# Split probabilities side by side: one product with the values per block of keys in a streaming attention kernel

## Chip, cores and metric

The kernel runs on one core of a Trainium2 chip. The metric is the device time of one execution in microseconds (us); a second time is the span of the profiled execution, from its first to its last instruction.

## What is computed

One layer of a streaming encoder, for 1024 new rows of a prompt group and 64 rows of a sample group, model width 1024, float32. One normalised input goes through one combined projection; three groups of heads share it (eight "forgetting attention" heads of width 64, a pooling mixer, four heads that attend to 256 memory tokens); gates and one output projection close the layer. Of the reference, the part that the change touches:

```python
def fox_attend(q, k, v, Fq, Fk, qpos, kpos):
    s = jnp.einsum('bqhd,bkhd->bhqk', q, k).astype(jnp.float32) * SCALE
    bias = jnp.transpose(Fq, (0, 2, 1))[..., :, None] - jnp.transpose(Fk, (0, 2, 1))[..., None, :]
    s = jnp.where(kpos[None, :] <= qpos[:, None], s + bias, NEG)
    p = jax.nn.softmax(s, axis=-1).astype(v.dtype)
    return jnp.einsum('bhqk,bkhd->bqhd', p, v)

def mem_attend(qm, mk, mv):
    s = jnp.einsum('bqhd,bkhd->bhqk', qm, mk).astype(jnp.float32) * SCALE
    p = jax.nn.softmax(s, axis=-1).astype(mv.dtype)
    return jnp.einsum('bhqk,bkhd->bqhd', p, mv)
```

## The kernel before

**Split numbers.** Products that need float32 accuracy are made of float32r operands: a high part (a rounded copy, made on ACT) and a low part (the rest, by a subtraction on DVE or GpSimd, POOL in the profile). A projection is three products per block (high by high, high by low, low by high), the `pp` accumulators of the profile with `xh`, `xl`, `whi`, `wlo`.

**Attention units.** A prompt head is worked in four units `fox_unit(h, c)` of 256 queries; unit c sees 256(c+1) keys. Scores go into `s`, softmax on DVE and ACT gives two probability tiles of 128 queries (`P` or `Q` by their width). Then, for each pair of key blocks `kp`, from the last down, TensorE transposes up to four 128x128 blocks into `pt`; `pt_split` makes the high part `phi` (ACT) and the low part `plo` (DVE); four products of 256 columns add up in the accumulator `o`. In the last pair (`kp == c`) the later key block lies wholly in the future of the first 128 queries: its transpose is left out, and two memsets on POOL put zeros there. The values `vs` hold their high part in one half of the 128 columns and their low part in the other, so one product gives both halves; `finish` adds the two halves of partitions (ACT copies one to `ot`, DVE adds) and stores the sum through `cat` to `catd` in memory. `mem_unit` does the same once per unit for the memory heads, with the values in `vm`. There are 8 x 4 prompt units with 1 to 4 pairs each (80 pairs, 32 of them last ones) and 4 x 4 memory units.

**Order.** Heads come in the order of a string, `f0 f1 f2 f3 m0 m1 m2 m3 f4 .. f7`, with projections of later tiles written behind each head as filler. A planner (`Planner`) takes the whole program, gives every operation a cost of its own (for a float32r product 0.008 us and 0.000435 us per column, at least 0.108), and writes out a fixed order for each engine by list scheduling: on TensorE, operations that write `s`, `pt` or `o` go first among those ready at one time. All engines then work their queues in that order. `q` and `k` of a pair of heads go through memory (`qd`, `kd`) and are loaded again (`qa`, `qb`, `ks`). When the last projection is done, `w_out` is loaded into the buffers of the split input, and the output projection runs over nine row tiles.

**Buffers.** PSUM: two each of `pp`, `s`, `pt`, `o`, one bank (512 float32 columns) each. In SBUF `phi`, `plo`, `ot` have two buffers, `cat` three. All loads and nearly all stores are issued by SP's queue.

In the trace nearly every instruction carries line 251, the line on which the planner emits; so one goes by tiles.

Of the kernel before, what the change touches and what calls it, by code (L numbers as in the profile page):

```python
# [7 lines left out]
F32 = mybir.dt.float32  # L8
F32R = mybir.dt.float32r
BF16 = mybir.dt.bfloat16  # L10
AF = mybir.ActivationFunctionType
ALU = mybir.AluOpType
AX = mybir.AxisListType

P = 128
# [256 lines left out]
def tile_hymba_step(  # L272
# [6 lines left out]
    nc = Planner(tc.nc, tc)  # L279
    PSUM = bass.MemoryType.PSUM  # L280

    def pool(name, bufs, space=None, to=ctx):
        kw = {} if space is None else {"space": space}
        return _Pool(nc, to.enter_context(tc.tile_pool(name=name, bufs=bufs, **kw)))
# [11 lines left out]
    def nm(s):  # L296
        uid[0] += 1
        return f"{s}_{uid[0]}"

    def pst():  # L300
        return ps.tile([P, 512], F32, tag="s", name=nm("s"))
# [10 lines left out]
    def otile():  # L312
        return po.tile([P, 512], F32, tag="o", name=nm("o"))

    def mm(out, lhsT, rhs, start, stop):
        nc.tensor.matmul(out, lhsT=lhsT, rhs=rhs, start=start, stop=stop)

    def half(par):
        return slice(64 * par, 64 * par + 64), slice(64 - 64 * par, 128 - 64 * par)
# [7 lines left out]
    catd = [dram.tile([D, 256 if c < 4 else NSA], F32, name=f"catd{c}") for c in range(5)]  # L327
# [138 lines left out]
    def vacc():  # L466
        vt_n[0] += 1
        return (ppt, pst, ppt, pst, otile, ptt, pst)[vt_n[0] % 7]()
# [183 lines left out]
    def small_halves():  # L652
        return sp.tile([P, 2, 512], F32R, tag="hm", name=nm("hm"), bufs=2)
# [36 lines left out]
    with st:  # L690
# [79 lines left out]
        for t, (wh, wl) in enumerate(wm):  # L770
            acc = vacc()
# [12 lines left out]
            hl = small_halves()  # L784
# [4 lines left out]
        for t in range(2):  # L789
            acc = vacc()  # L790
            c = slice(t * P, t * P + P)
# [19 lines left out]
    ap_ = pool("ap", 2)  # L811

    def small(shape, tag):
        return ap_.tile(shape, F32, tag=tag, name=nm(tag), bufs=6)
# [14 lines left out]
    def q_part(q, c):  # L829
        t = q[c in (2, 3)]  # L830
        c0, n = ((0, 256), (256, 256), (0, 256), (256, 256), (512, P))[c]
        return t[:, 0, c0 : c0 + n], t[:, 1, c0 : c0 + n]

    def score(out, q, qs, kst, ks0, n):
        mm(out, q[0][:, qs], kst[:, ks0 : ks0 + n], True, False)
        mm(out, q[1][:, qs], kst[:, ks0 : ks0 + n], False, True)

    def nbt(n):
        tag, w = ("nb", 512) if n <= 512 else ("nc", NPR)
        return ap_.tile([P, w], F32, tag=tag, name=nm(tag))  # L840

    def ptile(n=1024):
        tag, w, bufs = ("P", 512, 4) if n <= 512 else ("Q", 1024, 3)
        return ap_.tile([P, w], F32, tag=tag, name=nm(tag), bufs=bufs)

    def softmax_tail(Pt, m, rows, n, rs, src=None):
        nc.scalar.activation(
            Pt[:rows, :n], Pt[:rows, :n] if src is None else src, AF.Exp, bias=m,
            scale=-1.0 if src is None else 1.0, accum_out=rs[:rows],
        )  # L850
# [3 lines left out]
    def rs_col(c, head, i=0):  # L854
        return rsum[:, c, 12 * i + head : 12 * i + head + 1]
# [8 lines left out]
        nc.vector.tensor_copy(rt[:n, :m], tp[:n, :m])  # L864
        nc.sync.dma_start(rsd[c, :n, :m], rt[:n, :m])

    def pt_split(src, a, b):
        hi = ap_.tile([P, 512], F32R, tag="phi", name=nm("phi"))
        lo = ap_.tile([P, 512], F32R, tag="plo", name=nm("plo"))
        nc.scalar.copy(hi[:, a:b], src[:, a:b])  # L870
        nc.vector.tensor_tensor(lo[:, a:b], src[:, a:b], hi[:, a:b], op=ALU.subtract)
        return hi, lo

    def finish(acc, par, row0, t0, n):
        r, o = half(par)
        rows = slice(row0 + 64 * par, row0 + 64 * par + 64)
        t = ap_.tile([P, 256], F32, tag="ot", name=nm("ot"))
        nc.scalar.copy(t[r, :n], acc[o, :n])
        cat = ap_.tile([P, 256], F32, tag="cat", name=nm("cat"), bufs=3)
        nc.vector.tensor_tensor(cat[r, :n], acc[r, :n], t[r, :n], op=ALU.add)  # L880
        nc.sync.dma_start(catd[t0 // 256][rows, :n], cat[r, :n])

    def fox_load(h):
        par = h % 2
# [12 lines left out]
    def fox_unit(h, c, ks, vs, q):  # L897
        par = h % 2
        j = h // 2
        nk = 256 * (c + 1)  # L900
        nb = nbt(nk)
        r0 = 8 * c * (c + 1) + h * (2 * c + 2)
        nc.sync.dma_start(
            nb[:, :nk],
            gpd[r0 : r0 + 2 * c + 2, :].rearrange("t p -> (t p)").unsqueeze(0).to_broadcast([P, nk]),
        )
        bm = ap_.tile([P, P], F32, tag="bm", name=nm("bm"))
        nc.gpsimd.tensor_tensor(bm, nb[:, nk - 256 : nk - P], mask, op=ALU.add)
        nc.gpsimd.tensor_tensor(nb[:, nk - P : nk], nb[:, nk - P : nk], mask, op=ALU.add)
        q = q_part(q, c)  # L910
        pts = []
        for i in (0, 1):
            n = 256 * c + 128 * (i + 1)
            Pt = ptile(n)
            prev = BIG
            step = 320 if n == 640 else 512
            for a in range(0, n, step):
                w = min(step, n - a)
                wc = max(w, 256)
                s = pst()  # L920
                score(s[:, :wc], q, slice(P * i, P * i + P), ks, a, wc)
                d = n - P if i == 0 else n
                segs = [(a, min(a + w, d), nb)] if a < d else []
                if i == 0 and a + w == n:
                    segs.append((d, n, None))
                for b0, b1, src in segs:
                    m = small([P, 1], "m")
                    nc.vector.tensor_tensor_reduce(
                        out=Pt[:, b0:b1], in0=s[:, b0 - a : b1 - a],
                        in1=bm if src is None else nb[:, b0:b1],  # L930
                        scale=-1.0, scalar=prev, op0=ALU.add, op1=ALU.min, accum_out=m,
                    )
                    prev = m
            softmax_tail(Pt, prev, P, n, rs_col(c, h, i))
            pts.append(Pt)
        acc = otile()
        for kp in reversed(range(c + 1)):
            last = kp == c
            tp = ptt()
            for jj, kt in enumerate((2 * kp + 1, 2 * kp)):  # L940
                for i in (0, 1):
                    if last and jj == 0 and i == 0:
                        continue
                    nc.tensor.transpose(
                        tp[:, jj * 256 + i * P : jj * 256 + i * P + P],
                        pts[i][:, kt * P : kt * P + P], ident,
                    )
            hi, lo = pt_split(tp, P if last else 0, 512)
            if last:
                nc.gpsimd.memset(hi[:, 0:P].bitcast(F32), 0.0)  # L950
                nc.gpsimd.memset(lo[:, 0:P].bitcast(F32), 0.0)
            for jj, kt in enumerate((2 * kp + 1, 2 * kp)):
                for si, s in enumerate((hi, lo)):
                    mm(
                        acc[:, :256], vs[:, kt, :], s[:, jj * 256 : jj * 256 + 256],
                        last and jj == 0 and si == 0, kp == 0 and jj == 1 and si == 1,
                    )
        finish(acc, par, j * P, 256 * c, 256)

    def fox_sample(h, ks, raw, q):  # L960
        par = h % 2
# [60 lines left out]
    def mem_unit(h, c, km, vm, q):  # L1022
        par = h % 2
        j = h // 2
        q = q_part(q, c)
        s = pst()
        for i in (0, 1):
            score(s[:, i * 256 : i * 256 + 256], q, slice(P * i, P * i + P), km, 0, 256)
        m = small([P, 2], "m2")
        sv = s.rearrange("p (a b) -> p a b", a=2)  # L1030
        nc.vector.tensor_reduce(out=m, in_=sv, axis=AX.X, op=ALU.max, negate=True)
        Pt = ptile(512)
        for i in (0, 1):
            softmax_tail(
                Pt[:, i * 256 :], m[:, i : i + 1], P, 256, rs_col(c, 8 + h, i),
                src=s[:, i * 256 : i * 256 + 256],
            )
        tp = ptt()
        for kt in (0, 1):
            for i in (0, 1):  # L1040
                nc.tensor.transpose(
                    tp[:, kt * 256 + i * P : kt * 256 + i * P + P],
                    Pt[:, i * 256 + kt * P : i * 256 + kt * P + P], ident,
                )
        hl = pt_split(tp, 0, 512)
        acc = otile()
        for kt in (0, 1):
            for si in (0, 1):
                mm(
                    acc[:, :256], vm[:, kt, :], hl[si][:, kt * 256 : kt * 256 + 256],  # L1050
                    kt == 0 and si == 0, kt == 1 and si == 1,
                )
        finish(acc, par, 768 + j * P, 256 * c, 256)

    def mem_sample(h, km, raw, q):
        par = h % 2
# [406 lines left out]
```

## Time and profile before

| what | value |
|---|---|
| time, median of 3 runs | 606.6 us (604.79 to 608.34) |
| time of the profiled execution | 606.42 us |
| its span | 604.6 us |
| TensorE (PE) busy | 570.9 us, 94% of the span, 3815 matmuls |
| DVE, ACT, POOL busy | 336.1, 291.7, 219.9 us |

The profiled execution lies 0.2 us under the median, and 1.8 us of it lie outside the span. Busy time of matmuls is modelled and overlaps from one to the next, so what a matmul costs is read from the distance of starts, not from its length.

### The profile page before, as it was taken

Reading aid. Unit: us, or ns where it says so; the run is one execution under the profiler, and the core shown is the slowest. Engines: PE = TensorE matmul, PEld = TensorE weight load, DVE = VectorE, ACT = ScalarE, POOL = GpSimd, SP = SyncE. Lnnn points to the kernel's source line nnn. Section 1 sums busy time; section 2 is a strip of 40 time slices with the busy share of each in tenths; the row PEclk is TensorE's granted clock in tenths of the full one; section 3 lists DMA queues with packets and bytes.
Section 4 is the critical chain, followed back from the end, with each engine's and each line's share of the span. In section 5 each row is a group of like instructions: output and inputs, shape, how many; then the busy total and the mean of one; then the engine's idle time right before and its main releaser. Section 6 shows DMA issues by size and latency. Waiting matters only on the chain.

```text
span 604.6 us, 11202 instructions
## 1 busy us (share of the span) xinstructions
PE 570.9 (94%) x3815; PEld 522.4 (86%) x3815; DVE 336.1 (56%) x822; ACT 291.7 (48%) x675; POOL 219.9 (36%) x356
## 2 busy tenths in 40 slices
PE   7899999999999999999999999999999759898994
PEld 5899998989989999989999888989998648897894
DVE  5774521113778787647598636753365644535534
ACT  6653721211777877778488526741243333212212
POOL 2401373464746442123466533321114551311210
PEclk9899999999999999999999999999999978999998
DMA  8998745479996975596768668533245495684621
GB/s 311 328 329 289 233 126 205 139 275 283 330 342 214 342 233 144 159 340 212 248 180 293 219 203 267 186 89 117 80 141 173 137 233 138 200 232 153 207 105 70
DMA packets 99764, 128.59 MB, mean 213 GB/s; under 512 B 30931, under 2 KB 71675, under 8 KB 98171
## 3 DMA queue, kind: packets, MB, share of 16 engines
q1 hardware_dynamic: 99418, 127.61, 65.7%
q8 instruction: 30, 0.49, 0.3%
q10 hardware_dynamic: 288, 0.27, 0.1%
q14 instruction: 28, 0.22, 0.1%
HBM read 87.52 MB, written 40.33 MB: 211 GB/s over the span
## 4 chain that ended last, share of the span: by engine, by line
PE 77%; DMA 9%; DVE 6%; ACT 3%; issue 2%; POOL 2%; SPq 1%; DVEq 0%; POOLq 0%; ACTq 0%
PE pp L251 49%; PE s L251 12%; PE o L251 9%; PE pt L251 7%; DMA nat<-in_xn_dram 2%; DMA xr<-in_xT_dram 1%; DMA nc<-gpd 1%; DVE xt L251 1%; DMA xt<-in_xn_dram 1%; DVE gr L251 1%; DMA wr<-in_wv_dram 1%; DMA kd<-hl 1%; SPq L251 1%; DVE s L251 1%; DMA ks<-kd 1%
## 5 line engine op out<-in xcount | busy, mean ns | idle before, releaser
L251 PE MATMUL pp<-xh,whi 128*128 128x320 f32 (+2 forms) x480 | 149.3, 333 | 3.3 <-DVE kr L251 1.6
L251 PE MATMUL pp<-xh,wlo 128*128 128x512 f32 (+2 forms) x480 | 148.4, 332 | 0.0
L251 PE MATMUL pp<-xl,whi 128*128 128x320 f32 (+2 forms) x480 | 147.8, 329 | 0.0
L251 POOL TENSOR_TENSOR wlo<-wr,whi 128x512 fp32r<-128x512 f32 (+2 forms) x44 | 60.1, 1386 | 110.8 <-ACT whi L251 94.3
L251 PEld LDWEIGHTS pp<-xh,whi 128*128 128x128 f32 x480 | 88.3, 189 | 11.3 <-DVE gr L251 2.2
L251 PEld LDWEIGHTS pp<-xh,wlo 128*128 128x128 f32 x480 | 88.3, 188 | 6.0
L251 PEld LDWEIGHTS pp<-xl,whi 128*128 128x128 f32 x480 | 88.4, 189 | 5.0
L251 PE MATMUL pp<-wh,chi 128*128 128x256 f32 (+1 forms) x208 | 65.7, 332 | 14.1 <-DVE chi L251 7.9
L251 DVE TENSOR_TENSOR plo<-pt,phi 128x512 fp32r<-128x512 f32 (+1 forms) x96 | 60.8, 642 | 20.7 <-ACT phi L251 16.1
L251 ACT CAST phi<-pt 128x512 fp32r<-128x512 f32 (+1 forms) x96 | 51.7, 550 | 30.3 <-PE pt L251 16.6
L251 PE MATMUL pp<-wl,chi 128*128 128x256 f32 (+1 forms) x208 | 65.4, 328 | 0.0
L251 PE MATMUL pp<-wh,clo 128*128 128x256 f32 (+1 forms) x184 | 56.7, 324 | 0.0
L251 PEld LDWEIGHTS pp<-wh,chi 128*128 128x128 f32 x208 | 39.7, 194 | 19.3 <-DVE chi L251 8.1
L251 PE MATMUL o<-plo,vs 128*128 128x256 f32 x160 | 49.9, 324 | 0.0
L251 ACT CAST whi<-wr 128x1024 fp32r<-128x1024 f32 (+1 forms) x25 | 24.6, 983 | 51.8 <-PE pp L251 49.5
L251 PE MATMUL o<-phi,vs 128*128 128x256 f32 x160 | 47.5, 305 | 0.0
L251 PE MATMUL pt<-ident,Q 128*128 128x128 f32 x248 | 47.3, 272 | 0.0
L251 POOL TENSOR_TENSOR P<-P,P 128x512 f32<-128x512 f32 x17 | 22.2, 1319 | 66.4 <-DVE P L251 58.5
L251 ACT ACTIVATE Q<-Q,m 128x576 f32<-128x576 f32 (+4 forms) x40 | 38.0, 950 | 13.2 <-DVE m L251 13.1
L251 PEld LDWEIGHTS pp<-wl,chi 128*128 128x128 f32 x208 | 39.6, 193 | 3.5
L251 PE MATMUL s<-ks,qb 128*128 128x512 f32 (+3 forms) x128 | 37.9, 374 | 0.4 <-DVE m L251 0.3
L251 PEld LDWEIGHTS pp<-wh,clo 128*128 128x128 f32 x184 | 34.3, 190 | 3.3 <-DVE clo L251 0.7
(239 smaller groups left out, 1221.2 us busy)
## 6 DMA issues: line engine op xcount, KB each, us to landing
qd<-hl SPq DMA_DIRECT2D x24, 576.0 KB, 6.3
wr<-in_wt_dram SPq DMA_DIRECT2D x20, 512.0 KB, 3.7
qa<-qd SPq DMA_DIRECT2D x12, 640.0 KB, 6.3
ks<-kd SPq DMA_DIRECT2D x8, 800.0 KB, 7.4
qb<-qd SPq DMA_DIRECT2D x12, 512.0 KB, 4.8
P<-catd SPq DMA_DIRECT2D x17, 256.0 KB, 3.0
nat<-in_xn_dram SPq DMA_DIRECT2D x8, 512.0 KB, 7.8
kd<-hl SPq DMA_DIRECT2D x16, 256.0 KB, 5.2
```

Source lines behind the costliest of these rows:

```text
L251: getattr(getattr(self.nc, op.eng), op.fn)(*op.args, **op.kw)
```

## The change

The two parts stand side by side in one tile `phl`, for each of the four 128-column blocks of a pair first the high, then the low one. One product of 512 columns per key block then gives four sums (two query blocks, high and low) in four quarters of the accumulator `o`, which now fills its bank. In the last pair the earlier key block goes first, over all 512 columns, and the later one only over the 256 columns of the second query block; the memsets are gone. `finish` now works on 512 columns in its copy (ACT) and its addition (DVE, in place in `ot`), and POOL adds the high and the low quarter into `cat`, which has two buffers. The counts of transposes, splits and stores stay.

```diff
-    def pt_split(src, a, b):
-        hi = ap_.tile([P, 512], F32R, tag="phi", name=nm("phi"))
-        lo = ap_.tile([P, 512], F32R, tag="plo", name=nm("plo"))
-        nc.scalar.copy(hi[:, a:b], src[:, a:b])
-        nc.vector.tensor_tensor(lo[:, a:b], src[:, a:b], hi[:, a:b], op=ALU.subtract)
-        return hi, lo
-
-    def finish(acc, par, row0, t0, n):
+    def pt_split(src, b0):
+
+        hl = ap_.tile([P, 4, 2, P], F32R, tag="phl", name=nm("phl"))
+        v = src.rearrange("p (b t) -> p b t", b=4)[:, b0:]
+        hi, lo = hl[:, b0:, 0, :], hl[:, b0:, 1, :]
+        nc.scalar.copy(hi, v)
+        nc.vector.tensor_tensor(lo, v, hi, op=ALU.subtract)
+        return hl.rearrange("p b s t -> p (b s t)")
+
+    def finish(acc, par, row0, t0):
         r, o = half(par)
         rows = slice(row0 + 64 * par, row0 + 64 * par + 64)
-        t = ap_.tile([P, 256], F32, tag="ot", name=nm("ot"))
-        nc.scalar.copy(t[r, :n], acc[o, :n])
-        cat = ap_.tile([P, 256], F32, tag="cat", name=nm("cat"), bufs=3)
-        nc.vector.tensor_tensor(cat[r, :n], acc[r, :n], t[r, :n], op=ALU.add)
-        nc.sync.dma_start(catd[t0 // 256][rows, :n], cat[r, :n])
+        t = ap_.tile([P, 512], F32, tag="ot", name=nm("ot"))
+        nc.scalar.copy(t[r], acc[o])
+        nc.vector.tensor_tensor(t[r], acc[r], t[r], op=ALU.add)
+        cat = ap_.tile([P, 256], F32, tag="cat", name=nm("cat"))
+        v = t.rearrange("p (i s q) -> p i s q", i=2, s=2)
+        nc.gpsimd.tensor_tensor(
+            cat[r].rearrange("p (i q) -> p i q", i=2), v[r, :, 0, :], v[r, :, 1, :], op=ALU.add
+        )
+        nc.sync.dma_start(catd[t0 // 256][rows, :], cat[r])
...
-            hi, lo = pt_split(tp, P if last else 0, 512)
-            if last:
-                nc.gpsimd.memset(hi[:, 0:P].bitcast(F32), 0.0)
-                nc.gpsimd.memset(lo[:, 0:P].bitcast(F32), 0.0)
-            for jj, kt in enumerate((2 * kp + 1, 2 * kp)):
-                for si, s in enumerate((hi, lo)):
-                    mm(
-                        acc[:, :256], vs[:, kt, :], s[:, jj * 256 : jj * 256 + 256],
-                        last and jj == 0 and si == 0, kp == 0 and jj == 1 and si == 1,
-                    )
-        finish(acc, par, j * P, 256 * c, 256)
+            hl = pt_split(tp, 1 if last else 0)
+            for jj in (1, 0):
+                c0 = 256 if last and jj == 0 else 0
+                mm(
+                    acc[:, c0:], vs[:, 2 * kp + 1 - jj, :], hl[:, jj * 512 + c0 : jj * 512 + 512],
+                    last and jj == 1, kp == 0 and jj == 0,
+                )
+        finish(acc, par, j * P, 256 * c)
...
-        hl = pt_split(tp, 0, 512)
+        hl = pt_split(tp, 0)
         acc = otile()
         for kt in (0, 1):
-            for si in (0, 1):
-                mm(
-                    acc[:, :256], vm[:, kt, :], hl[si][:, kt * 256 : kt * 256 + 256],
-                    kt == 0 and si == 0, kt == 1 and si == 1,
-                )
-        finish(acc, par, 768 + j * P, 256 * c, 256)
+            mm(acc, vm[:, kt, :], hl[:, kt * 512 : kt * 512 + 512], kt == 0, kt == 1)
+        finish(acc, par, 768 + j * P, 256 * c)
```

## Rows read from the trace of the kernel before

**Rows 1.** The page: its head and part 1, for each engine busy time, share of the span, number of instructions, on one line.

```profile
span 604.6 us, 11202 instructions
...
PE 570.9 (94%) x3815; PEld 522.4 (86%) x3815; DVE 336.1 (56%) x822; ACT 291.7 (48%) x675; POOL 219.9 (36%) x356
```

**Rows 2.** The table by stretches of time (start:end in us, length, then busy us and instructions of each engine, TensorE's granted clock, DMA share, GB/s).

```profile
180.00:200.00 20.00, 19.91 (x142) 18.53 (x142) 16.08 (x50) 14.79 (x36) 13.24 (x30) 1.00 0.74 241
300.00:320.00 20.00, 19.67 (x148) 18.91 (x147) 18.20 (x61) 15.16 (x37) 13.80 (x27) 1.00 0.67 190
...
340.00:360.00 20.00, 18.97 (x126) 17.14 (x125) 9.04 (x15) 6.35 (x14) 10.06 (x17) 1.00 0.53 177
360.00:380.00 20.00, 18.25 (x128) 16.90 (x128) 12.41 (x42) 12.04 (x30) 6.31 (x13) 1.00 0.72 228
...
480.00:500.00 20.00, 10.35 (x35) 7.60 (x34) 12.08 (x16) 6.86 (x11) 11.51 (x9) 0.80 0.95 236
```

**Rows 3.** The chain of work that ended last, in order of time (start us, length us, what).

```profile
346.53 0.21 POOL phi L251
...
348.38 2.73 POOL wlo L251 x2
...
355.19 5.24 DMA kd<-hl
...
360.50 4.33 DMA ks<-kd
...
401.05 32.64 PE pp L251 x201
...
458.83 14.95 PE pp L251 x72
...
481.13 4.02 DMA wr<-in_wout_dram
```

**Rows 4.** TensorE's groups of matmuls with shapes kept apart, those that write the accumulator `o` from the split probabilities (count, busy us, mean ns of one as the profiler models it, idle before).

```profile
L251 PE MATMUL o<-plo,vs 128*128 128x256 f32 x160 | 49.9, 324 | 0.0
...
L251 PE MATMUL o<-phi,vs 128*128 128x256 f32 x160 | 47.5, 305 | 0.0
...
L251 PE MATMUL o<-plo,vm 128*128 128x256 f32 x32 | 8.6, 289 | 0.0
L251 PE MATMUL o<-phi,vm 128*128 128x256 f32 x32 | 8.6, 291 | 0.0
```

**Rows 5.** TensorE's matmuls in order of time (start us, modelled length us). From the first to the second row stand eight 512-column products one behind the other, then three rows of the mixed stream, and from the last but one to the last 38 rows of 256 columns, so 37 steps.

```profile
334.71 0.40 PE L251 MATMUL pp<-xh,whi 128*128 128x512 f32 x1
...
336.57 0.28 PE L251 MATMUL o<-plo,vs 128*128 128x256 f32 x1
...
340.04 0.37 PE L251 MATMUL o<-phi,vs 128*128 128x256 f32 x1
340.24 0.27 PE L251 MATMUL pt<-ident,Q 128*128 128x128 f32 x1
340.27 0.37 PE L251 MATMUL o<-plo,vs 128*128 128x256 f32 x1
...
355.05 0.28 PE L251 MATMUL pp<-xl,whi 128*128 128x256 f32 x1
...
359.45 0.28 PE L251 MATMUL pp<-xh,wlo 128*128 128x256 f32 x1
```

**Rows 6.** The timeline of all engines, two products and the weight load (PEld) between them.

```profile
308.03 0.28 PE L251 MATMUL o<-phi,vs 128*128 128x256 f32 x1
308.04 0.19 PEld L251 LDWEIGHTS o<-plo,vs 128*128 128x128 f32 x1
308.15 0.28 PE L251 MATMUL o<-plo,vs 128*128 128x256 f32 x1
```

**Rows 7.** Groups of instructions of ACT, DVE and POOL, shapes kept apart (count, busy us, mean ns of one, idle before and its releasers).

```profile
L251 ACT CAST phi<-pt 128x512 fp32r<-128x512 f32 x64 | 37.2, 587 | 22.4 <-PE pt L251 9.3 <-PE o L251 5.9 <-issue 4.7
...
L251 ACT COPY ot<-o 64x256 f32<-64x256 f32 x48 | 17.6, 366 | 6.7 <-PE o L251 5.6
...
L251 DVE TENSOR_TENSOR plo<-pt,phi 128x512 fp32r<-128x512 f32 x64 | 43.6, 687 | 15.3 <-ACT phi L251 12.7 <-POOL bm L251 1.3 <-issue 0.9
L251 DVE TENSOR_TENSOR cat<-o,ot 64x256 f32<-64x256 f32 x48 | 20.0, 419 | 11.1 <-ACT ot L251 7.8 <-DMA catd<-cat 2.8
...
L251 POOL MEMSET phi<- 128x128 f32 x32 | 6.4, 205 | 24.9 <-PE o L251 16.0 <-PE pt L251 4.6 <-DVE plo L251 2.0
...
L251 POOL TENSOR_TENSOR s<-s 64x256 f32<-64x256 f32 x4 | 2.9, 735 | 0.3
```

**Rows 8.** The tile `cat` between 240 and 300 us: its instructions (min/median/max ns), the waits before them (us, times), and the store's time to landing.

```profile
L251 DVE TENSOR_TENSOR cat<-o,ot x17: 403/421/430, 248.9 to 297.9; 64x256 f32<-64x256 f32 x17
...
  DMA catd<-cat: 2.8, 2
...
DMA to landing us min/median/max: 2.6/4.3/5.4
```

## Prediction

> **What bounds the kernel now.** I read the profile's front page first: TensorE is busy 94% of the span, and no other engine above 56% [rows 1]. A busy share of modelled, overlapping matmuls proves little, so the table by stretches comes next. In the attention stretches (about 160 to 455 us) TensorE is busy 19.9 and 19.7 of 20 us, with the projections between the attention's products; its idle time there gathers in one place, 1.03 + 1.75 = 2.8 us between 340 and 380 us. The other hole is 9.65 us between 480 and 500 us, after the attention [rows 2]. Then the chain that ended last: from 401 us it is TensorE's projections for 32.6 us, again for 15.0 us from 458.8, then the load of the output weights at 481 us. Around 346 to 365 us it leaves TensorE and runs over POOL (a memset of `phi`, two weight splits), the store of `kd` and the load of `ks` [rows 3]. So two things are to be seen. From 160 to about 477 us the time is the sum of TensorE's work, and whatever is taken out of its stream comes off the end, because the output weights can go into the buffers of the split input only when the last projection is done. And attention runs ahead of the projections: TensorE still has those 201 + 72 projection products to do when most of the attention is over, so a later end of a unit is covered by them, if the fixed order puts them in the right place.
>
> **TensorE's part.** The trace has 160 + 160 products of 256 columns with `vs` and 32 + 32 with `vm` [rows 4], four in each of 80 + 16 pairs. What one costs is the distance of starts: from 334.71 to 336.57 us eight products of 512 columns pass, 1.86 / 8 = 0.2325 us each; from 355.05 to 359.45 us 37 of 256 columns, 4.40 / 37 = 0.119 us each [rows 5]. Two of 256 (0.238) against one of 512 (0.2325) is only 0.0055 us less: the engine is paid by columns, not by instructions.
> - Pairs of key blocks with all columns: 80 - 32 = 48 prompt pairs and 16 memory pairs, two mergers each: 64 x 2 x 0.0055 = 0.7 us.
> - Last pairs: before 4 x 0.119 = 0.476 us, after 0.2325 + 0.119 = 0.3515; 32 x 0.1245 = 4.0 us.
> Sum 4.7 us. The bounds: if a merger saves nothing, only the 256 columns are left, 32 x 0.119 = 3.8 us. In the mixed stream a transpose and a product together take 0.23 us (340.04 to 340.27) [rows 5], that is 0.11 for a transpose of 128 columns, more than its columns are worth; so there something other than columns may be paid. If each removed instruction were worth that 0.11 beyond its columns, the 192 removed ones would give 192 x 0.11 = 21 us. I take the lower view, because where no transpose stands the products are already paid by columns, and because the weight load for the second product starts at 308.04 us, 0.01 us behind the first product, and the second product starts at 308.15, 0.12 behind the first [rows 6]: a load runs under a product of 256 columns.
>
> The Trainium skill, page "TensorE: Matmul & The Clock Gate", section "What overlaps and what doesn't", says that a weight load overlaps a running product only where their row groups differ; here all are full height, and by that rule each of 192 loads left out would be paid back in full (its section "LDWEIGHTS (loading the stationary operand)" gives columns / 1.2 ns, so by estimate 107 ns each and some 20 us). The start just shown speaks against it.
>
> **The other engines' part** [rows 7].
> - ACT: the copy grows from 256 columns (0.366 us) to 512; the nearest row is the `phi` copy of 512 columns out of PSUM, 0.587. 48 x 0.22 = 10.6 us more.
> - DVE: the addition grows from 0.419 us to that of the 512-column `plo` subtraction, 0.687. 48 x 0.27 = 12.9 us more.
> - POOL: 48 new additions of 64x256; the nearest row is such an addition at 0.735 us: 35.3 us. Gone are 64 memsets of 0.205 us, 13.1 us. Net 22.2 us more.
> - The splits write every second block of 128 columns instead of one stretch. No row here has that form from PSUM; between nothing and, say, a tenth of 0.587 and 0.687 us for 96 splits, 0 to 12 us on ACT and DVE together. I take nothing.
> All this is costed at zero for the end. The cover is TensorE's stream. In the first heads DVE, at 16.08 of 20 us, gets some four finishes more work, 1.1 us, and stays under 87%; the cover is thinnest at 300 to 320 us, where DVE is busy 18.20 of 20 us [rows 2] and the same 1.1 comes on top. If that cover is gone, a unit's accumulator comes free about 0.22 + 0.27 = 0.5 us later; with two accumulators a wait of that size could show in some of the 48 units, at most 24 us if in all. I take zero, as 201 projection products follow when attention is nearly over.
>
> What is queued behind the new additions: on POOL the mask additions for later units, the `hl` splits and the weight splits; on SP each store of `cat`, about 1 us later than before, with the loads behind it. With two `cat` buffers in place of three, it is POOL that waits for a store to land (median 4.3 us); before, DVE did so twice, for 2.8 us in all, in the memory heads [rows 8]. With 17 of these stores in 49 us (2.9 us apart), two buffers of 0.7 + 4.3 us each allow one in 2.5, and the issue on SP's queue comes on top: barely enough. A wait of POOL there delays `k`'s split, and no product of TensorE at once.
>
> Sum: 606.4 - 4.7 = 601.7 us for the profiled execution; it lies 0.2 under the median, so 601.9 us against 606.6.
>
> **The rivals.**
> - *Taken back by waits (same).* The columns go, but the new order puts as much idle time into TensorE's stream, or the hole at 480 us is set by the transfer of the weights (DMA share 0.95 [rows 2]) rather than by the last projection. For it: the order is planned anew from estimated costs. Against: the chain enters that load from the projections. Time: 601.9 plus 2 to 6, so 604 to 608. Chance 0.26.
> - *POOL becomes the bound (slower).* Place: 346 to 365 us, where the chain already runs over POOL to the store of `kd` and the load of `ks`, while TensorE idles. Sixteen memory units bring POOL 16 x 0.735 = 11.8 us more, eight units of the next two heads 8 x (0.735 - 0.41) = 2.6, together 14.4, and waits for `cat`. Each us by which the split of the last `k` slips beyond POOL's free time is a us of TensorE without work. It decides from a slip of 4.7 + 3 = 7.7 us on; a slip of 12 gives 606.6 - 4.7 + 12 = 614. Against: POOL is busy only 10.06 of 20 us there, and the two memsets on that very chain go. Chance 0.11.
> - *Weight loads are the price (much faster).* 606.6 - 21 = 586 us, or about 592 if only the products between transposes gain. Chance 0.05.
>
> **How the numbers follow.** The forecast, 601.9 with its own range of 599 to 604.5 (the bounds 3.8 and 4.7, and some 2 us of newly arranged waits on either side), has 0.58. A difference under 0.5% (3 us) is about what a measurement of this kernel can't tell from none, so faster means below 603.6 and slower above 609.6. Faster: 0.52 of the forecast's 0.58, all of the third rival's 0.05, 0.02 of the first: 0.59. Slower: 0.11. Same: the rest, 0.30. The range of 597 to 609 leaves out the third rival and most of the second.
>
> **What the changed profile would show.** 192 matmuls fewer, 3623; 32 of 256 columns and 160 of 512 into `o`; in steady stretches 0.23 us from start to start for these, not less. TensorE's busy time 4 to 5 us lower, the last attention product and the first output product earlier by about that. The copy of 512 columns near 0.59 us, the addition near 0.69, POOL's addition near 0.74. Wrong would be: more idle time of TensorE in 340 to 380 us with POOL on the chain, DVE without a gap in the prompt heads, or starts closer than 0.2 us in the mixed stream.

## The result, and the profile after

| | before | after |
|---|---|---|
| time, median of 10 runs each on one chip | 608.37 us | 603.47 us (601.18 to 605.88) |
| ratio after to before, 95% interval | | 0.9934 (0.9913 to 0.9955) |
| profiled execution, its span | 606.42, 604.6 us | 604.07, 602.3 us |

By the ratio the change makes the kernel faster by 0.66%, some 4.0 us (2.7 to 5.3 by its interval; the two medians lie 4.9 us apart), where the forecast was 4.7. The profiled execution shows only 2.3 us of it: single executions of one kernel lie up to 0.4% to either side of its median, and this one lost part of the gain in the output stage. TensorE's granted clock between 480 and 500 us was 0.67 of full, before 0.80, and ten steps between products of 512 columns took 0.43 us each there, before seven. So below the length of the attention stretch is read beside the ratio: from the first to the last start of a product of split probabilities (`phl`; before, `phi` and `plo`) with `vs` into `o`, in the one profiled execution of each kernel.

The page's head and part 1, for [rows 1]:

```profile
span 602.3 us, 10773 instructions
...
PE 566.0 (94%) x3623; PEld 508.2 (84%) x3623; DVE 349.5 (58%) x822; ACT 300.2 (50%) x675; POOL 244.1 (41%) x340
```

TensorE does 4.9 us less, in 192 matmuls fewer; DVE, ACT and POOL do 13.4, 8.5 and 24.2 us more. The table by stretches, for [rows 2] (columns as there), with 160 to 180 us added:

```profile
160.00:180.00 20.00, 17.64 (x110) 15.02 (x109) 14.62 (x36) 13.17 (x29) 12.57 (x18) 1.00 0.99 325
180.00:200.00 20.00, 19.96 (x128) 17.56 (x127) 17.08 (x49) 16.76 (x41) 12.13 (x23) 1.00 0.71 220
...
300.00:320.00 20.00, 19.50 (x128) 17.30 (x127) 18.37 (x49) 16.90 (x41) 17.22 (x26) 1.00 0.77 243
...
340.00:360.00 20.00, 20.00 (x130) 17.71 (x129) 12.43 (x25) 12.29 (x24) 9.01 (x12) 1.00 0.89 264
360.00:380.00 20.00, 20.00 (x138) 18.84 (x137) 14.57 (x46) 14.07 (x33) 7.76 (x14) 1.00 0.67 207
...
480.00:500.00 20.00, 13.28 (x40) 9.99 (x41) 10.04 (x13) 5.09 (x8) 9.46 (x7) 0.67 0.84 208
```

Idle time has moved. The 2.8 us that TensorE stood still between 340 and 380 us are gone. In their place it loses 2.36 us between 160 and 180 us (1.49 in a second execution, after_again below), where it was busy throughout before:

```profile
160.00:180.00 20.00, 20.00 (x143) 18.39 (x142) 15.59 (x45) 16.41 (x38) 11.70 (x20) 1.00 1.00 353
```

The groups, shapes kept apart, that answer to [rows 4] and [rows 7] (count, busy us, mean ns, idle before and its releasers):

```profile
L251 PE MATMUL o<-phl,vs 128*128 128x512 f32 x128 | 50.2, 442 | 0.0
L251 DVE TENSOR_TENSOR phl<-pt,phl 128x512 fp32r<-128x512 f32 x64 | 43.5, 687 | 11.1 <-ACT phl L251 10.3
L251 ACT CAST phl<-pt 128x512 fp32r<-128x512 f32 x64 | 37.1, 586 | 18.8 <-PE pt L251 12.3 <-PE o L251 5.1 <-PE s L251 1.0
L251 POOL TENSOR_TENSOR cat<-ot 64x256 f32<-64x256 f32 x48 | 36.2, 754 | 60.7 <-DVE ot L251 34.3 <-issue 12.3 <-DMA catd<-cat 5.0
L251 DVE TENSOR_TENSOR ot<-o,ot 64x512 f32<-64x512 f32 x48 | 32.8, 685 | 13.4 <-ACT ot L251 12.8
L251 ACT COPY ot<-o 64x512 f32<-64x512 f32 x48 | 27.9, 582 | 11.1 <-PE o L251 8.3 <-POOL cat L251 1.6
...
L251 PE MATMUL o<-phl,vs 128*128 128x256 f32 x32 | 9.7, 308 | 0.0
```

### The profile page after: what moved, and what is told of

The parts are those of the page before. It is cut to its first block, busy times and chain, and to the rows that moved or that the text cites. A ratio compares the mean times of both kernels' runs of the same rounds, so it can differ in the third digit from the quotient of the medians.

```text
span 602.3 us, 10773 instructions
## 1 busy us (share of the span) xinstructions
PE 566.0 (94%) x3623; PEld 508.2 (84%) x3623; DVE 349.5 (58%) x822; ACT 300.2 (50%) x675; POOL 244.1 (41%) x340
## 5 line engine op out<-in xcount | busy, mean ns | idle before, releaser
L251 DVE TENSOR_TENSOR phl<-pt,phl 128x512 fp32r<-128x512 f32 (+1 forms) x96 | 60.5, 642 | 13.2 <-ACT phl L251 12.2
L251 ACT CAST phl<-pt 128x512 fp32r<-128x512 f32 (+1 forms) x96 | 51.9, 550 | 24.2 <-PE pt L251 17.0
L251 POOL TENSOR_TENSOR cat<-ot 64x256 f32<-64x256 f32 x48 | 36.2, 754 | 60.7 <-DVE ot L251 34.3
L251 PE MATMUL o<-phl,vs 128*128 128x512 f32 (+1 forms) x160 | 55.3, 415 | 0.0
L251 DVE TENSOR_TENSOR ot<-o,ot 64x512 f32<-64x512 f32 x48 | 32.8, 685 | 13.4 <-ACT ot L251 12.8
L251 PEld LDWEIGHTS pt<-ident,Q 128*128 128x128 f32 x248 | 32.1, 140 | 7.4 <-issue 3.1
```

Source lines behind the costliest of these rows:

```text
L251: getattr(getattr(self.nc, op.eng), op.fn)(*op.args, **op.kw)
```

## The experiments

The kernel plans its own order, so an edit usually moves everything else too. Eight of these kernels therefore keep the order planned for the changed kernel (planned costs are kept where the work is altered). skip_narrow is planned with the costs of before, skip_clean with its own, and the last two with another margin. Ratios are to the kernel before on the same chip; 0.001 is 0.6 us.

| kernel | ratio (95%) | attention stretch, us |
|---|---|---|
| before | 1 | 290.4 |
| after | 0.9934 (0.9913 to 0.9955) | 286.8 |
| after_again | 0.9935 (0.9911 to 0.9960) | 286.0 |
| cols_back | 0.9962 (0.9938 to 0.9986) | 287.6 |
| halves | 0.9916 (0.9891 to 0.9941) | 286.1 |
| skip_narrow | 0.9978 (0.9958 to 0.9997) | 288.9 |
| cat_memset | 0.9897 (0.9862 to 0.9931) | 283.8 |
| finish_half | 0.9879 (0.9840 to 0.9917) | 282.9 |
| finish_twice | 1.0322 (1.0286 to 1.0359) | 310.2 |
| skip_clean | 1.0003 (0.9976 to 1.0030) | 290.1 |
| order_short | 0.9936 (0.9909 to 0.9963) | 288.1 |
| order_only | 0.9947 (0.9926 to 0.9967) | 287.3 |
| before_m36 | 0.9998 (0.9979 to 1.0018) | 290.4 |
| after_m36 | 0.9928 (0.9905 to 0.9952) | 285.2 |

### Are the instructions or the columns the price?

**after_again** is the changed kernel once more, as a yardstick.

> The changed kernel once more, as a yardstick for the three beside it. Both theories: a ratio to the kernel before of 0.993, about 4 us faster.

0.9935, as the first time. **halves** issues each product of 512 columns as two of 256, at the same place in the order:

```diff
+fn(out[:, :256], **{**kw, "rhs": rhs[:, :256], "stop": False})
+fn(out[:, 256:], **{**kw, "rhs": rhs[:, 256:], "start": False, "stop": stop})
```

> The changed kernel in its own order, but each of the 160 products of 512 columns is issued as two of 256 columns with the same values, so 160 instructions and weight loads come back and no column does. Theory 'columns': 160 x 0.0055 = 0.9 us slower than the changed kernel. Rival 'weight loads are the price': 160 x 0.11 = 17 us slower.

0.9916, inside the yardstick's interval: 160 more products and weight loads cost nothing that can be measured, so merging gave nothing that can be measured either.

**cols_back** lets the later block of a last pair run over 512 columns again:

```diff
-acc[:, c0:], vs[:, 2 * kp + 1 - jj, :], hl[:, jj * 512 + c0 : jj * 512 + 512],
+acc, vs[:, 2 * kp + 1 - jj, :], hl[:, j0 : j0 + 512],   # j0 = 512 if c0 else jj * 512
```

> The changed kernel in its own order on every engine, but the second product of each last pair streams all 512 columns again (the columns of the first query block are taken from the earlier key block, so the sums of that block are other than asked). Theory 'columns': 32 x 256 columns at 0.119 us for 256 come back, 3.8 us slower than the changed kernel, within 1.5 us of the kernel before. Rival 'the gain is a luckier order or fewer instructions': no more than 1 us slower than the changed kernel, since neither order nor count changes.

0.9962, that is 0.0027 or 1.6 us slower than after_again, where 32 x 0.1135 = 3.6 us of columns were put back. The sign is right, and less than half the size arrives, but by the two intervals the difference is good to 2.1 us only, so neither the 3.6 nor none is ruled out by it. What may have taken the rest is the question of the runs below.

**skip_narrow** is the kernel before, with the two products of the later block over 128 columns, after the earlier block's; memsets and planned costs stay. **skip_clean** also drops the memsets and is planned with the new costs.

```diff
-for jj, kt in enumerate((2 * kp + 1, 2 * kp)):
+for jj, kt in ((1, 2 * kp), (0, 2 * kp + 1)):
+    c0 = P if last and jj == 0 else 0
...
-            acc[:, :256], vs[:, kt, :], s[:, jj * 256 : jj * 256 + 256],
+            acc[:, c0:256], vs[:, kt, :], s[:, jj * 256 + c0 : jj * 256 + 256],
...
```

> The kernel before, with its two tiles and its old finish and its memsets, where in each last pair the earlier key block goes first and the two products of the later key block take only the 128 columns of the second query block: the block of zeros is left out without putting the parts side by side. If a product of 128 columns costs its columns (0.06 us), 64 x 0.06 = 3.8 us faster than before, as much as the change. If it costs as much as a transpose of 128 columns, 0.11 us, 64 x 0.01 = 0.6 us faster, no difference to be measured. If narrow products of this type are slower by column, as the three products of 64 columns in the trace of before at 354.34 to 354.83 us hint (0.11 to 0.13 us for a quarter of 256 columns), also no difference or slower.

> The kernel before with its two tiles and its short finish, the later key block of each last pair taken over 128 columns, and the memsets, whose zeros nobody reads, left out; planned anew with the planner's own cost of a 128-column product. Theory 'columns': TensorE's work falls by 64 x 0.06 = 3.8 us at most, as in the changed kernel, without any longer finish: ratio to the kernel before 0.990 to 0.996, at least as fast as the changed kernel. Rival 'the order decides': the ratio falls anywhere between 0.985 and 1.005 whatever the columns, and the idle time in the attention stretch tells why.

0.9978 and 1.0003: the same columns left out without the merging, and little or nothing gained. One reason is the price of a narrow product. TensorE's products in skip_narrow, and its weight loads in the same stretch:

```profile
306.67 0.28 PE L251 MATMUL o<-plo,vs 128*128 128x256 f32 x1
306.79 0.22 PE L251 MATMUL o<-phi,vs 128*128 128x128 f32 x1
306.85 0.28 PE L251 MATMUL o<-plo,vs 128*128 128x128 f32 x1
306.96 0.36 PE L251 MATMUL pp<-xl,whi 128*128 128x320 f32 x1
```

```profile
306.67 0.19 PEld L251 LDWEIGHTS o<-phi,vs 128*128 128x128 f32 x1
306.79 0.19 PEld L251 LDWEIGHTS o<-plo,vs 128*128 128x128 f32 x1
306.90 0.19 PEld L251 LDWEIGHTS pp<-xl,whi 128*128 128x128 f32 x1
```

The first of the two passes in 0.06 us, as its columns say, but the next product comes 0.11 us behind the second, because its weights start 0.11 us after those before. The two take 0.17 us, against 0.119 for the one product of 256 columns in the changed kernel. So 128 columns are too few to cover the load of the next such product, 256 are enough. Side by side pays here, by at most 32 x 0.05 = 1.6 us: nine of the 32 pairs in skip_narrow stand so, the others have a transpose between them or behind them, where this price can't be read off. The other reason in skip_clean is the order: the hole of [rows 2] is still there.

```profile
340.00:360.00 20.00, 18.75 (x126) 16.94 (x125) 9.44 (x16) 6.27 (x14) 10.67 (x15) 1.00 0.53 173
360.00:380.00 20.00, 18.07 (x128) 16.93 (x128) 12.07 (x42) 12.33 (x30) 6.22 (x12) 1.00 0.70 220
```

### What does the longer finish cost?

**finish_half** shortens the copy and the addition to 256 columns; **finish_twice** issues both twice; **cat_memset** puts a memset in place of POOL's addition. The order is that of after in all three. The sums of all three are other than asked; POOL adds the half tile of finish_half to itself.

```diff
-nc.scalar.copy(t[r], acc[o])
-nc.vector.tensor_tensor(t[r], acc[r], t[r], op=ALU.add)
+nc.scalar.copy(t[r, :256], acc[o, :256])                                  # finish_half
+nc.vector.tensor_tensor(t[r, :256], acc[r, :256], t[r, :256], op=ALU.add)
...
 fn(*op.args, **op.kw)                                                     # finish_twice
+if op.seq in self.twice: fn(*op.args, **op.kw)
...
-nc.gpsimd.tensor_tensor(cat[r]..., v[r, :, 0, :], v[r, :, 1, :], op=ALU.add)
+nc.gpsimd.memset(cat[r], 0.0)                                             # cat_memset
```

> The changed kernel in its own order, with the copy and the addition of the finish on 256 columns as before (the other half of the sums is left out; POOL adds the tile to itself). Theory 'costed at nothing', as in the prediction: within 1 us of the changed kernel, since TensorE's stream covers 0.5 us less per unit. Rival 'the finish costs': the accumulators come free 0.5 us earlier and the attention stretch gets 2 us shorter or more.

> The changed kernel in its own order, with the copy and the addition of the finish each issued twice (the sums are then other than asked): ACT 48 x 0.58 = 28 us and DVE 48 x 0.69 = 33 us more work. Theory 'cover': projections behind the attention hide it, within 2 us of the changed kernel. Rival 'the order is fixed': products that wait for a late part stop all behind them, so a good part of 48 x 1.27 = 61 us shows; by bounds 5 to 40 us slower.

> The changed kernel in its own order on every engine, with POOL's addition of the high and the low quarter replaced by a memset of the same tile (so that sum is left out: zeros are stored). Theory 'port': in the changed kernel DVE's subtraction of two operands in SBUF at 174.16 us took 2.60 us for two where its mean is 0.77 each, while POOL added into cat and split vs, and TensorE then waited 1.48 us; the new additions on POOL cost TensorE idle time through DVE. Without them the 2.9 us of idle time between 160 and 180 us shrink to under 1 and the attention stretch gets 1.5 to 3 us shorter than in the changed kernel. Rival 'hidden': no difference over 1 us, idle time in the same places.

0.9879, 1.0322 and 0.9897. Against after's 0.9934, the half finish gives back 3.3 us, the doubled one costs 23.6 us more, and POOL's addition alone is worth 2.2 us. By the intervals the first is good to 2.7 us and the last to 2.4, so the last is not clear of none by the ratio; its stretch is 2.2 to 3.0 us shorter than in the two executions of after. The 3.3 and the 2.2 are not to be added: finish_half keeps POOL's addition, and most of TensorE's idle time between 160 and 180 us goes in either run. The waits of TensorE, and the longest of DVE, in finish_twice from 160 to 480 us (total us, times, longest):

```profile
PE pt L253 <- DVE phl L253: 6.0, 8, 1.6
PE o L253 <- DVE phl L253: 4.9, 7, 1.0
PE o L253 <- DVE ot L255: 2.8, 6, 1.0
...
DVE ot L253 <- ACT ot L255: 18.5, 19, 3.0
```

Of these only the third line is the accumulator coming free late. The larger part, 10.9 us, is waiting for DVE's next `phl` subtraction. In eleven of these fifteen waits the subtraction stands right behind the two additions in DVE's fixed order, and the additions had often waited for ACT's copies.

POOL's addition works in another way. The timeline of after (of its rows those of DVE and POOL, and TensorE around the wait), then the same place in cat_memset, in cols_back and in finish_half:

```profile
174.16 2.60 DVE L251 SCALAR_TENSOR_TENSOR s<-s,winv,u 64x256 f32<-64x256 f32 x2
...
174.32 0.92 POOL L251 TENSOR_TENSOR cat<-ot 64x256 f32<-64x256 f32 x1 [0.88 <-DVE ot L251]
...
175.20 1.27 POOL L251 TENSOR_TENSOR vs<-vraw,vs 128x512 fp32r<-128x512 f32 x1
...
175.75 0.40 PE L251 MATMUL pp<-xl,whi 128*128 128x512 f32 x1
176.79 1.16 DVE L251 TENSOR_TENSOR phl<-pt,phl 128x512 fp32r<-128x512 f32 x2
...
177.63 0.41 PE L251 MATMUL pt<-ident,Q 128*128 128x128 f32 x2 [1.48 <-DVE phl L251]
```

```profile
172.47 0.30 POOL L251 MEMSET cat<- 64x256 f32 x1
...
173.25 0.98 DVE L251 SCALAR_TENSOR_TENSOR s<-s,winv,u 64x256 f32<-64x256 f32 x2
...
173.95 1.45 POOL L251 TENSOR_TENSOR vs<-vraw,vs 128x512 fp32r<-128x512 f32 x1 [1.18 <-ACT vs L251]
...
174.27 1.16 DVE L251 TENSOR_TENSOR phl<-pt,phl 128x512 fp32r<-128x512 f32 x2
...
175.10 0.41 PE L251 MATMUL pt<-ident,Q 128*128 128x128 f32 x2
```

```profile
172.18 2.60 DVE L251 SCALAR_TENSOR_TENSOR s<-s,winv,u 64x256 f32<-64x256 f32 x2
...
175.64 0.41 PE L251 MATMUL pt<-ident,Q 128*128 128x128 f32 x2 [0.66 <-DVE phl L251]
```

```profile
172.21 1.23 DVE L251 SCALAR_TENSOR_TENSOR s<-s,winv,u 64x256 f32<-64x256 f32 x2
172.37 0.79 POOL L251 TENSOR_TENSOR cat<-ot 64x256 f32<-64x256 f32 x1 [0.62 <-DVE ot L251]
...
173.32 1.30 POOL L251 TENSOR_TENSOR vs<-vraw,vs 128x512 fp32r<-128x512 f32 x1 [0.17 <-ACT vs L251]
```

Two DVE instructions with both inputs in SBUF take 2.60 us in after while POOL adds and then splits `vs`, 1.23 us in finish_half, where POOL adds but the split comes only as they end, and 0.98 us in cat_memset, where POOL's addition is not there. So the full 2.60 us need the addition and the split one behind the other. `phl` is that much later, and TensorE waits 1.48 us for it, most of the idle time at 160 to 180 us. In cols_back the same two take 2.60 us again, but TensorE, with more columns to stream, comes to that place later and waits only 0.66 us there: columns that the change removed had been cover. The Trainium skill, page "SBUF — State Buffer", section "Who interferes with whom", says that a DVE instruction with two SBUF inputs contends with a GpSimd instruction that reads SBUF, not with one that only writes it. The rows agree with the first half. For the second, the memset above is over before the pair begins; in before, at 332.95 us, one such instruction ran beside two memsets of POOL and took 0.49 us, as long as with POOL idle.

### What does the order give?

**order_short** keeps the arithmetic of the kernel before (high and low part one behind the other, the short finish, narrow products), without memsets, in the order planned for after. **order_only** does the same with 256 columns in the later block too, and so has before's amount of work on TensorE in after's order (the sums of its first queries are other than asked).

```diff
+nc.emit[op.seq] = [
+    ((acc[:, c0:256],), dict(
+        lhsT=w, rhs=hl[:, 512 * i + a + c0 : 512 * i + a + 256],
+        start=start and i == 0, stop=stop and i == 1,
+    ))
+    for i in (0, 1)
+]                                    # c0 = 0 throughout in order_only
```

> The arithmetic of the kernel before, with its finish on 256 columns and without memsets, the later key block of each last pair taken over 128 columns for the high and the low part; but every engine works in the order that the planner made for the changed kernel (POOL's addition falls out of that order). Theory 'order': what hid the longer finish in the changed kernel is its order; with the short finish in the same order the time falls under that of the finish cut to 256 columns (ratio 0.988) or level with it, since POOL's addition is gone too (2 us) and narrow products beside transposes cost some 1.6 us more: ratio 0.985 to 0.990. Rival 'columns alone decide': 0.993 as in the changed kernel, or 1.000 as in the version planned for itself.

> As the last one, but the later key block of each last pair is taken over 256 columns for each part, as in the kernel before (the columns come from the earlier key block, so the sums of the first queries are other than asked): all columns of the kernel before, its short finish, no memsets, in the order made for the changed kernel. Theory 'order': the order alone is worth 3 to 4.5 us, the idle time that stood between 340 and 365 us: ratio 0.992 to 0.996 and no such idle time. Rival 'the order is worth nothing': ratio 0.998 to 1.002.

0.9936 and 0.9947. With all the columns and the short finish of before, but after's order, order_only is 3.2 us faster than before, and the hole is gone:

```profile
340.00:360.00 20.00, 20.00 (x146) 18.70 (x145) 11.17 (x24) 11.59 (x24) 6.03 (x8) 1.00 0.89 268
360.00:380.00 20.00, 20.00 (x143) 19.13 (x142) 14.39 (x46) 13.54 (x32) 6.97 (x13) 1.00 0.64 197
```

Part of how the hole closes can be read: before, 1.2 us of it were a wait for the load of `ks`, which is issued some 5 us earlier in after's order and no longer waited for (SP's issue of the load in before, after and order_only):

```profile
361.43 0.35 SPq L251 DMA_DIRECT2D ks<-kd  x1
...
355.61 0.99 SPq L251 DMA_DIRECT2D ks<-kd  x2
...
355.06 1.01 SPq L254 DMA_DIRECT2D ks<-kd  x2
```

The step from before to order_only also leaves out the 64 memsets on POOL, two of which stood on the chain to that load [rows 3]. In skip_clean they are left out without after's order, and the hole stays, so they alone don't close it. So most of a gain of this size can be had without the change's arithmetic. order_short, which also leaves out the columns, does no better: its narrow products pay for their loads, as in skip_narrow (21 of its 32 pairs take 0.17 us), and it has one wait of its own:

```profile
PE o L254 <- DMA vraw<-in_cmv_dram: 1.6, 1, 1.6
```

**before_m36** and **after_m36** plan both kernels with the planner's margin at 0.36 in place of 0.40, to see how much of a difference is one lucky order.

```diff
-MARGIN = 0.4
+MARGIN = 0.36
```

> The kernel before, planned with 0.36 us instead of 0.40 for a result's way to TensorE: another order, nothing else. Theory 'the order is worth some us': the ratio differs from 1 by up to 0.008 either way. Rival 'orders are alike': within 0.002 of 1.

> The changed kernel planned with 0.36 us instead of 0.40: another order, nothing else. Theory 'the order is worth some us': its ratio to the kernel before differs from 0.993 by up to 0.008 either way. Rival 'orders are alike': 0.991 to 0.996.

0.9998 and 0.9928: both kernels stay where they were. after_m36 does so although it has a gap in that stretch (TensorE 18.42 of 20 us busy), so the missing hole alone doesn't decide. No kernel that does the whole computation is clearly faster than after: halves and after_m36 lie within its interval.

```profile
340.00:360.00 20.00, 18.42 (x123) 16.44 (x122) 12.77 (x28) 10.63 (x22) 6.94 (x11) 1.00 0.82 275
```

### The account

Four kernels in one order make a square:

| | later block over all columns | over half of them |
|---|---|---|
| short finish | order_only 0.9947, 287.3 us | finish_half 0.9879, 282.9 us |
| long finish | cols_back 0.9962, 287.6 us | after 0.9934, 286.8 us (again 0.9935, 286.0) |

The order, with the memsets, is worth 3.2 us (before to order_only). Leaving out the columns is worth 4.1 us where the finish is short, 1.7 us where it is long; the long finish costs 0.9 us where the columns are streamed, 3.3 us where they are not. By the upper way, -3.2 - 4.1 + 3.3 = -4.0 us. That sum closes by construction, and by the intervals each step is good to 1 to 3 us, so the ratios alone don't prove that columns and finish depend on each other. The stretches, which repeat better (286.8 and 286.0), show the same pattern: 4.4 against 0.8 to 1.6 us for the columns, 0.3 against 3.1 to 3.9 for the finish. And the traces show where it goes. The stretch as one window (columns as in [rows 2]), for before, order_only, finish_half, cols_back and after:

```profile
163.80:454.20 290.40, 287.05 (x2001) 266.26 (x2000) 189.54 (x497) 181.84 (x452) 110.69 (x215) 1.00 0.66 213
...
164.50:451.80 287.30, 286.27 (x2001) 266.39 (x1999) 191.70 (x497) 181.67 (x453) 99.69 (x155) 1.00 0.68 218
...
163.60:446.50 282.90, 281.86 (x1810) 252.74 (x1808) 191.85 (x497) 181.36 (x453) 129.11 (x203) 1.00 0.68 219
...
163.70:451.30 287.60, 285.78 (x1810) 254.45 (x1808) 205.10 (x497) 190.81 (x452) 134.35 (x202) 1.00 0.67 215
...
164.00:450.80 286.80, 282.67 (x1810) 252.44 (x1808) 203.95 (x497) 190.90 (x453) 134.78 (x202) 1.00 0.68 218
```

TensorE's busy time falls by 4.4 us from before to after. Its idle time, the length less the busy time, is 3.4 us before, 1.0 in order_only, 1.0 in finish_half, 1.8 in cols_back and 4.1 in after (3.4 in after_again). So the order takes 2.3 us of waits out, and the longer finish puts 2.4 to 3.1 in where the columns are gone, against 0.8 where they are streamed. These are single executions, so differences under 1 us among them say little. The square is not quite pure: order_only has two products for one and no addition on POOL. halves prices the first at nothing; the second is part of the long finish in cols_back and after, while finish_half has it.

## Why the prediction was right

The forecast was 601.9 us, 4.7 under its time; measured were 4.0 under. TensorE's busy time fell by 4.4 us in the attention stretch and by 4.9 in all, as the sum had it. That its idle time came out nearly level is luck: a cost that was put at nothing and a gain that was not in the sum cancelled within the noise.

- **What bounds the kernel: right.** What left TensorE's stream came off the end: the last attention product starts at 450.8 us in place of 454.2, the first output product at 484.95 in place of 488.16, 3.4 and 3.2 us earlier. So the hole before the output stage is set by the last projection, as the chain said [rows 3], and the loading of the weights, offered as an alternative in the first rival, didn't take the gain.
- **Columns, 4.0 us: right, as work of TensorE.** finish_half against order_only gives 4.1 us (good to 2.7), and there idle time stays the same. In the changed kernel itself they bring 1.7 (good to some 2), as waits take their place.
- **Merging, 0.7 us: too small to see.** halves shows no loss, and 0.7 us lies inside its interval.
- **Weight loads as the price (586 to 592): wrong here**, by the runs and not by [rows 6] alone. The Trainium skill, page "TensorE: Matmul & The Clock Gate", section "What overlaps and what doesn't", lets a weight load overlap a product only where row groups differ; 160 loads of full height were added in halves and the time did not rise, so the measurement decides against it for products of 256 columns.
- **Sizes on ACT, DVE and POOL: right.** 0.582, 0.685 and 0.754 us against 0.587, 0.687 and 0.735 [rows 7]; the splits into every second block take 0.586 and 0.687 us, as before, so that unknown was nothing.
- **"All this is costed at zero for the end": this step failed.** The longer finish costs 3.3 us (0.7 to 6 by the intervals). The view by stretches had TensorE at 19.9 of 20 us, and I took that for cover. It says that TensorE had work, not that it had work to spare: the columns that were removed were part of the cover. What is late next was also named too narrowly. I priced an accumulator coming free 0.5 us later; finish_twice shows that DVE's next subtraction, behind the additions, is the larger part there. And POOL's addition was weighed against POOL's own free time and the `cat` buffers alone, not against DVE, which it slows together with the split behind it. The bounds written down, 0 to 24 us, hold the value; zero was the wrong end to rest on.
- **The order, not in the sum: 3.2 us.** It was named only as a danger, "the new order puts as much idle time into TensorE's stream". The new order did put waits in at 160 to 180 us, but it took as much or more out, at 340 to 380. This gain and the cost of the finish are each uncertain by more than their difference of 0.1 us.
- **POOL becomes the bound (614): wrong.** It was to show between 346 and 365 us, and just there TensorE is busy 20.00 of 20 us. At 300 to 320 us POOL goes from 13.80 to 17.22 of 20 us, and TensorE is idle for 0.50 us there, before 0.33.

What stays open: whether the better order is a consequence of the change, as the planner counts a longer finish and fewer columns, or chance. Four plans of before's kind (before, before_m36, skip_narrow, skip_clean) have the hole, two of after's kind are both faster; that is too few to tell.

## What to carry to other kernels

Work taken from the engine that is the bound can also take cover from the engines beside it: a cost that is hidden before must be priced in the kernel after. A square of four runs (each part alone, both, neither) can show such an interaction, if the idle time of the bound engine is read in each beside the total. In a kernel that plans its own order, run the old arithmetic in the new order before crediting the arithmetic. And when an addition moves to POOL, look for DVE instructions with two SBUF inputs that run at that moment and for what POOL does next, not only for free time on POOL.

## What the runs showed of the hardware that was not expected

- Two DVE instructions of 64x256 with both inputs in SBUF took 2.60 us beside POOL's addition and split, 0.98 us without the addition. The mean of one over the sixteen is 774 ns in after, 607 in cat_memset, and was 674 before; in finish_half, with the addition, it is 685. Of the 2.7 us between after and cat_memset 1.6 come from this one place:

```profile
L251 DVE SCALAR_TENSOR_TENSOR s<-s,winv,u 64x256 f32<-64x256 f32 x16 | 12.4, 774 | 0.3
```

```profile
L251 DVE SCALAR_TENSOR_TENSOR s<-s,winv,u 64x256 f32<-64x256 f32 x16 | 9.7, 607 | 0.3
```

- A product of 128 columns can start 0.06 us ahead of the next, but two in a row take 0.17 us. In the attention stretches of before, skip_narrow, order_short and after, the weight loads of two products into `o` never start closer than 0.107 us; a product of 256 columns (0.119 us) stands just above that. A load for a transpose can come closer, 0.055 us behind one for `o`. Ahead of the result the 0.11 us of a transpose [rows 5] was read as something beyond columns that a removed product might give back. halves shows that products of 256 columns pay no such thing; whether the transpose's 0.11 us has the same cause is not shown.
- A finish doubled in 48 units puts 48 x (0.582 + 0.685) = 61 us more on ACT and DVE together, which in after are busy 50 and 58% of the span; 23.6 us of it reach the end.
